# Four column groups in the first feed-forward, seven buffers for modulation weights, first weight splits issued earlier

## The chip, the cores and the metric

The kernel runs on one core of one Trainium2 chip. The metric is the device time of one launch in microseconds: a median of several runs, and beside it one execution that was profiled, to which every row below belongs. The core has a matrix engine (TensorE, written PE in the rows, with its weight loads as PEld), a vector engine (DVE), a scalar engine (ACT), GpSimd (POOL) and a sync engine (SP). Here POOL and SP mostly issue DMA transfers.

## The reference, cut to what matters

Two transformer blocks run over 512 rows of width 1024 in float32. The first has two layers. Each layer has a mixer (pooling and attention in layer 0, an mLSTM in layer 1) and a SwiGLU feed-forward, and both are modulated by columns that come from a product of the condition `c` with `ada_w`:

```python
# the modulation of one layer: six parts of 1024 columns, from ada_w[layer], a 1024 x 6144 matrix
def modulate(h, shift, scale):
    return h * (1.0 + scale[:, None, :]) + shift[:, None, :]

def swiglu(h, w1, w3, w2):                     # hidden width 2816 = 22 blocks of 128
    return (jax.nn.silu(h @ w1) * (h @ w3)) @ w2

# the second block starts from the memory as well:
x = x + memory_cross_attention(rmsnorm(x, mem_q_norm[l]), rmsnorm(mem, mem_kv_norm[l]),
                               mem_w_q[l], mem_w_kv[l], mem_w_o[l])
```

The second block (a feed-forward, a mixer, the memory attention, a second feed-forward) is not touched by the change, but a piece of its memory work is done early, inside the first block.

## The kernel before, in words

**Numbers and products.** The residual stream `x` is held as eight tiles of 128x512 (128 of the 1024 columns on the partitions, the 512 rows beside them). A float32 operand is split into a high and a low part, and each product takes three matmuls: high by high, low by high, high by low (`mm3`, L160 to L162). Weights are split the same way on the fly. SP loads a raw piece of about 1 MB into one of two buffers `raw` (L185), ACT copies the high part `wh` (L151), and DVE subtracts to get the low part `wl` (L130). PE needs `wh` for the first two matmuls of a product and `wl` for the third.

**The stages that the change touches**, in order of time: the end of layer 0's mixer with its output projection (`ev_w_out`, from about 200 us), the first feed-forward (about 255 to 640 us), and the start of the mLSTM's input projection (`od_w_in`, from about 640 us).

**Feed-forward.** `ffn` works through the 22 blocks of the hidden width in groups. For each group it makes the hidden tiles `g` of all its blocks, and then it runs the second weight matrix `w2` over the group: eight output tiles of 128x512, each the sum over the group's blocks, and each added to its tile of `x` by one DVE operation in `resid` (L908). So there are eight such additions for each group. The groups are (0,8), (8,8) and (16,6), written as first block and number. Most of the first product is done by a scheme of seven smaller products for two halves of the rows and two blocks of columns (`uprod`, matmuls L621 to L623 of 128x256), whose weight sums `sm` and inputs `h`, `hx` (`form`, L554) are made on DVE and ACT. The first four blocks' products of the first group are plain ones (`plain`, `plain_half`, L160 to L162).

**Modulation beside it.** `ada_wide` (L436) computes the modulation columns that are needed later as 16 jobs of eight tiles. POOL issues a load of 128x512 floats (256 KB) into a buffer `araw` (L449), DVE multiplies by the condition and accumulates into `acc` (L477, L479), PE sums over the partitions with four one-column matmuls (L455), and DVE writes the column (L464, L466). There are three buffers, and a load is issued two tiles ahead of its use. This work is a generator: the stages around it call it a few steps at a time (`some(side, n)`), from `evac` of the output projection, from `ffn` and from its `evac`.

**Between two stages.** `beside` (L1941) steps through the eight tiles of `modulated_forms` (L520: multiply by `rstd` on DVE, shift on ACT, split on both) or of `modulated` (L510, L512), and after every tile it lets some of the memory's work run (`fill`). The first weight splits of the stage that follows are issued once all eight tiles are done.

**The memory.** `mem_load` reads the normalised memory (`md`) back into tiles at the end of the first feed-forward, and `mem_split` splits it into `mh` and `ml`.

**What sets the order.** Python writes the instructions in the order of these loops, and a scheduler in the framework then places each on its engine's queue by its own priorities. So moving a call also moves instructions of other calls. Each engine works through its queue in order.

Of the kernel before, what the change touches and what calls it, by code (L numbers as in the profile page):

```python
# [50 lines left out]
class Net:  # L51
# [4 lines left out]
                     u=3, pm=2, acc=2, araw=3, dv=2),  # L56
        "ffn0": dict(ps=dict(wb=2, wg=2, ad=1), hx=15, w1=2, w3=4, w22=4, sm=1, g=16, s=3, u=2, c=5, acc=2, araw=3),
        "ffn": dict(ps=dict(wb=2, wg=2, ad=1), hx=15, w1=2, w3=4, w22=4, sm=1, g=16, s=4, u=4, c=6),
# [4 lines left out]
        "mem": dict(ps=dict(s=2, pt=2, po=1), r=4, k=8, q=16, p=7, pt=8),  # L63
    }

    adape = ((1, 0, 0, 0), (1, 1, 0, 0))
# [373 lines left out]
    def ada_wide(self, jobs):  # L440
# [26 lines left out]
        todo = iter([(j, k) for j in range(len(jobs)) for k in range(KT)])  # L467
        got = [load(*next(todo)) for _ in range(2)]
        for j, job in enumerate(jobs):
            acc = self.t(tag="acc")  # L470
            for k in range(KT):
                t = got.pop(0)
                jk = next(todo, None)
                if jk:
                    got.append(load(*jk))
                if k == 0:
                    nc.vector.tensor_scalar(out=acc, in0=t, scalar1=self.cond[:, 0:1], scalar2=None, op0=ALU.mult)  # L477
                else:
# [162 lines left out]

    def ffn_units(self, w1, c1, w3, c3):

        return [[dict(w=w, c=c + j * P, j=j - j0, up=up) for j in range(j0, j0 + gn, 2)
                 for up, w, c in ((False, w1, c1), (True, w3, c3))] for j0, gn in self.GROUPS]

# [34 lines left out]

    GROUPS = ((0, 8), (8, 8), (16, 6))

    def ffn(self, hs, pair, units, w2, normed, scale, after, last=None, then=None, side=None):

# [79 lines left out]

        for gi, (j0, gn) in enumerate(self.GROUPS):
            us, gs, prev = units[gi], [None] * gn, None
# [6 lines left out]
            for i, u in enumerate(us[i0:], i0):  # L774
# [25 lines left out]
                if side:  # L800
                    self.some(side, 1)
                prev = u
# [7 lines left out]
            self.mms(ps0, t0, gs, 3, gn - 2)  # L810
            t1 = next(tiles)
            ps1 = self.ps()
            self.mms(ps1, t1, gs, 0, 3)
            pss = {0: (ps0, gn - 2), 1: (ps1, 3)}

            def evac(n, ps):
                self.resid(n, ps, scale, rstd)
                if gi == len(self.GROUPS) - 1:
                    after(n)
                elif side:  # L820
                    self.some(side, 2)
            nxt = t0
            for n in range(D // P):
                if last and gi == len(self.GROUPS) - 1 and n == 6:
# [879 lines left out]

    def mem_load(self, tag="g"):
# [144 lines left out]
    def run(self):  # L1850
        a = self.a
        self.nform = self.ssn = 0
        self.eraw = self.esplit = None
        self.setup()
        self.load_x()
        pre0, hs0 = [], []
        up0, up, up1, up2 = (self.ffn_units(a[n][i], 0, a[m][j], c) for n, i, m, j, c in (
            ("ffn_w1", 0, "ffn_w3", 0, 0), ("ffn_w1", 1, "ffn_w3", 1, 0),
            ("ffn1_w_gu_2", 0, "ffn1_w_gu_2", 0, NFF * P), ("ffn2_w_gu_2", 0, "ffn2_w_gu_2", 0, NFF * P)))
        for layer in range(2):  # L1860
            ins, fill = [], []

            def evac(n, ps):
# [11 lines left out]
            if layer == 0:  # L1875
# [4 lines left out]
                with self.phase(**self.PH["ffn0"]):  # L1880
# [7 lines left out]
                    self.ss_fin()  # L1888
                    self.beside(self.modulated_forms(0, 1, pre1, ins), fill[0], (1, 0, 1, 0, 1, 0, 1, 0))

                    def then(n):
                        if n == 0:
                            self.mem_load("hx")
# [10 lines left out]
                    self.ffn(ins, lambda p: pre1[2 * p:2 * p + 2], up0, a["ffn_w2"][0], False, gate, after, then=then,  # L1904
                             side=side)
                    self.drain(side)
                    self.ss_fin()
                    self.beside(self.modulated(1, 0, pre0, hs0), fills[0], (1, 0, 1, 0, 1, 0, 1, 0))
            else:
                with self.phase(**self.PH["mlstm"]):  # L1910
                    mix = self.mlstm(hs0)
                with self.phase(**self.PH["ffn"]):
                    self.mem_load()
                    for i in range(4):
# [26 lines left out]

    def beside(self, g, fill, counts):

        for n in counts:
            next(g)
# [122 lines left out]
```

## Time and profile before

| | |
|---|---|
| runs | 2481.32 us median of 3 (2479.53 to 2482.18) |
| profiled execution | 2470.95 us, span on the core 2469.2 us |
| PE busy | 2371.5 us of the span, 96% |
| DVE, ACT, POOL busy | 1884.7, 1277.9, 229.1 us |

The profiled execution lies 10.4 us (0.4%) below the median, and 1.75 us of it lie outside the span. PE is busy nearly all the time, so what can be won or lost is the 4% in which it is idle, and the time in which it works at the lower of its clock's two levels (2.4 GHz, shown as 1.00, and 1.2 GHz, shown as 0.50). Both are found in the timeline's idle times, printed in brackets as idle before the instruction and what ended it, and in the windows' column PEclk.

### The profile page before, as it was taken

Reading aid. Unit: us, or ns where it says so; the run is one execution under the profiler, and the core shown is the slowest. Engines: PE = TensorE matmul, PEld = TensorE weight load, DVE = VectorE, ACT = ScalarE, POOL = GpSimd, SP = SyncE. Lnnn points to the kernel's source line nnn. Section 1 sums busy time; section 2 is a strip of 40 time slices with the busy share of each in tenths; the row PEclk is TensorE's granted clock in tenths of the full one; section 3 lists DMA queues with packets and bytes.
Section 4 is the critical chain, followed back from the end, with each engine's and each line's share of the span. In section 5 each row is a group of like instructions: output and inputs, shape, how many; then the busy total and the mean of one; then the engine's idle time right before and its main releaser. Section 6 shows DMA issues by size and latency. Waiting matters only on the chain.

```text
span 2469.2 us, 36653 instructions
## 1 busy us (share of the span) xinstructions
PE 2371.5 (96%) x14418; PEld 2082.1 (84%) x14418; DVE 1884.7 (76%) x3064; ACT 1277.9 (52%) x2136; POOL 229.1 (9%) x361
## 2 busy tenths in 40 slices
PE   7898899999999989999999999999999999999997
PEld 5567898979788768989898999988888788899996
DVE  7887987968687767868678787876778765978686
ACT  3564643526557756536366444455555534645453
POOL 2332112120002220000000000001011200000000
PEclk9999999999999999999999999999999999999999
DMA  9417555453333324333323333322111221233232
GB/s 303 132 54 221 170 171 192 160 186 108 118 98 95 98 67 143 113 103 103 103 86 103 103 104 103 103 94 84 52 52 52 86 86 61 94 103 110 96 102 70
DMA packets 242821, 276.37 MB, mean 112 GB/s; under 512 B 8124, under 2 KB 227132, under 8 KB 242648
## 3 DMA queue, kind: packets, MB, share of 16 engines
q1 hardware_dynamic: 232408, 240.46, 30.5%
q0 software_dynamic: 10240, 33.56, 4.2%
q8 instruction: 113, 1.85, 0.3%
q14 instruction: 60, 0.49, 0.1%
HBM read 268.47 MB, written 5.53 MB: 111 GB/s over the span
## 4 chain that ended last, share of the span: by engine, by line
PE 54%; DVE 6%; ACT 2%; issue 1%; DMA 0%; POOL 0%; DVEq 0%; ACTq 0%; POOLq 0%
PE ps L160 9%; PE ps L161 9%; PE ps L162 8%; PE ps L621 8%; PE ps L623 8%; PE ps L622 8%; DVE wl L130 1%; ACT wh L151 1%; PE ps L266 1%; PE ps L264 1%; PE ps L265 1%; PE ps L1606 1%; DVE ga L1618 0%; DVE h L130 0%; DVE w L130 0%
## 5 line engine op out<-in xcount | busy, mean ns | idle before, releaser
L151 ACT ACTIVATE wh<-raw 128x1024 fp32r<-128x1024 f32 (+1 forms) x312 | 321.0, 1030 | 457.4 <-PE ps L161 286.8
L130 DVE TENSOR_TENSOR wl<-raw,wh 128x1024 fp32r<-128x1024 f32 (+1 forms) x312 | 373.4, 1197 | 74.0 <-ACT wh L151 71.7
L161 PE MATMUL ps<-g,wh 128*128 128x512 f32 (+1 forms) x780 | 296.4, 380 | 0.0
L162 PE MATMUL ps<-g,wl 128*128 128x512 f32 (+1 forms) x748 | 288.1, 385 | 5.8 <-DVE wl L130 5.8
L160 PE MATMUL ps<-g,wh 128*128 128x512 f32 (+1 forms) x748 | 288.7, 386 | 0.9 <-ACT wh L151 0.7
L161 PE MATMUL ps<-h,wh 128*128 128x512 f32 x704 | 282.2, 401 | 1.6 <-DVE h L936 1.2
L160 PE MATMUL ps<-h,wh 128*128 128x512 f32 x688 | 278.8, 407 | 2.9 <-ACT c L151 1.2
L162 PE MATMUL ps<-h,wl 128*128 128x512 f32 x688 | 271.9, 398 | 9.3 <-DVE wl L130 9.2
L621 PE MATMUL ps<-hx,wh 128*128 128x256 f32 x960 | 272.5, 284 | 1.3 <-ACT c L151 0.7
L621 PE MATMUL ps<-h,w 128*128 128x256 f32 x960 | 272.6, 284 | 0.3 <-ACT c L151 0.3
L623 PE MATMUL ps<-h,w 128*128 128x256 f32 x960 | 271.5, 283 | 0.7 <-DVE w L130 0.7
L623 PE MATMUL ps<-hx,wl 128*128 128x256 f32 x960 | 272.2, 284 | 0.0
L622 PE MATMUL ps<-h,w 128*128 128x256 f32 x960 | 271.5, 283 | 0.0
L622 PE MATMUL ps<-hx,wh 128*128 128x256 f32 x800 | 226.7, 283 | 0.0
L151 ACT ACTIVATE c<-ps 128x256 f32<-128x256 f32 (+1 forms) x344 | 130.3, 382 | 132.9 <-PE ps L623 132.3
L621 PEld LDWEIGHTS ps<-hx,wh 128*128 128x128 f32 x960 | 184.7, 192 | 2.1 <-ACT wh L151 1.2
L621 PEld LDWEIGHTS ps<-h,w 128*128 128x128 f32 x960 | 184.4, 192 | 2.1 <-ACT c L151 1.1
L623 PEld LDWEIGHTS ps<-h,w 128*128 128x128 f32 x960 | 184.2, 192 | 1.1 <-DVE w L130 1.1
L622 PEld LDWEIGHTS ps<-h,w 128*128 128x128 f32 x960 | 184.4, 192 | 0.9
L623 PEld LDWEIGHTS ps<-hx,wl 128*128 128x128 f32 x960 | 184.8, 192 | 0.0
L162 PEld LDWEIGHTS ps<-g,wl 128*128 128x128 f32 x748 | 141.9, 190 | 35.2 <-DVE wl L130 7.7
L161 PEld LDWEIGHTS ps<-g,wh 128*128 128x128 f32 x780 | 148.0, 190 | 27.1 <-issue 0.5
(445 smaller groups left out, 5596.6 us busy)
## 6 DMA issues: line engine op xcount, KB each, us to landing
raw<-in_ffn_w_dram SPq DMA_DIRECT2D x60, 1024.0 KB
raw<-in_ffn_w_gu_dram SPq DMA_DIRECT2D x44, 1024.0 KB
araw<-in_ada_w_dram POOLq DMA_DIRECT2D x128, 256.0 KB, 4.1
araw<-in_ada_w_dram SPq DMA_DIRECT2D x16, 1024.0 KB
raw<-in_ffn_w_down_dram SPq DMA_DIRECT2D x16, 1024.0 KB
raw<-in_w_in_dram SPq DMA_DIRECT2D x14, 1024.0 KB
raw<-in_od_w_in_dram SPq DMA_DIRECT2D x12, 1024.0 KB
raw<-in_mem_w_kv_dram SPq DMA_DIRECT2D x8, 1024.0 KB
```

The lines of the kernel that those rows point to most:

```text
L130: nc.vector.tensor_tensor(out=lo, in0=src, in1=hi.bitcast(F32), op=ALU.subtract)
L151: r = nc.scalar.activation(out=out, in_=in_, func=func, **kw)
L160: mm(out, wh, xh, start=first, stop=False)
L161: mm(out, wh, xl, start=False, stop=False)
L162: mm(out, wl, xh, start=False, stop=last)
L264: mm(out, xh[:, sl], wh[:, k], start=(half == 0 and i % 2 == 0 and k == 0), stop=False)
L265: mm(out, xl[:, sl], wh[:, k], start=False, stop=False)
L266: mm(out, xh[:, sl], wl[:, k], start=False, stop=(half == 1 and i % 2 == 1 and k == 3))
L621: mm(out, wh[:, k], xh, start=(m in (1, 5) and k == 0), stop=False, skip_group_check=True)
L622: mm(out, wh[:, k], xl, start=False, stop=False, skip_group_check=True)
L623: mm(out, wl[:, k], xh, start=False, stop=(k == 3), skip_group_check=True)
L1606: nc.tensor.matmul(ps[:, c * P:(c + 1) * P], lh[:, c * P:(c + 1) * P], rh[:, c * P:(c + 1) * P], start=True, stop=True)
```

## The change

- The first feed-forward's groups become (0,6), (6,6), (12,6), (18,4): `GROUPS0`. The other feed-forwards keep `GROUPS`. The number of matmuls is the same.
- `ada_wide` has seven `araw` buffers and loads six tiles ahead. It yields after every tile (before: every second one), and its callers ask for other numbers of steps. The room comes from `g`, which goes from 16 buffers to 12.
- `beside` takes a place and a function. Ahead of tile 5 (of 8) it issues the first weight load and split of the first feed-forward (`plain_begin`), ahead of tile 5 the first two of `od_w_in`, and ahead of tile 6 those of layer 1's feed-forward.
- `form` gives the modulated tiles of the first feed-forward buffers of `h` first and of `hx` later (`formskip`), and the memory's high parts lie in `hx`.

```diff
-        "ffn0": dict(... hx=15, ... g=16, s=3, u=2, c=5, acc=2, araw=3),
+        "ffn0": dict(... hx=15, ... g=12, s=3, u=2, c=5, acc=2, araw=7),
...
+    GROUPS = ((0, 8), (8, 8), (16, 6))
+    GROUPS0 = ((0, 6), (6, 6), (12, 6), (18, 4))
...
-        got = [load(*next(todo)) for _ in range(2)]
+        got = [load(*next(todo)) for _ in range(6)]
...
-                if tail and k == 1:
+                if tail and k == 0:
                     ps = sums(tail[0])
-                elif tail and k == 5:
+                elif tail and k == 3:
                     result(ps, *tail[1])
-                if k % 2:
-                    yield
+                yield
...
-        n = self.nform % 32
+        n = (self.nform + self.formskip) % 32
...
+    def plain_begin(self, us):
+        self.uload(us[0])
+        self.plain_half(us[0], 0)
...
                 if side:
-                    self.some(side, 1)
+                    self.some(side, 2)
...
-            self.mms(ps0, t0, gs, 0, 3)
+            k3 = min(3, gn - 2)
+            self.mms(ps0, t0, gs, 0, k3)
...
                 elif side:
-                    self.some(side, 2)
+                    self.some(side, 3)
...
-    def mem_tiles(self, tag="g"):
+    def mem_tiles(self, tag="hx"):
...
                 if layer == 0:
-                    self.some(side, 2)
+                    self.some(side, (4, 4, 3, 3, 3, 3, 4, 4)[n])
...
-                    self.beside(self.modulated_forms(0, 1, pre1, ins), fill[0], (1, 0, 1, 0, 1, 0, 1, 0))
+                    self.beside(self.modulated_forms(0, 1, pre1, ins), fill[0], (1, 0, 1, 0, 1, 0, 1, 0), 5,
+                                lambda: self.plain_begin(up0[0]))
...
-                             side=side)
+                             side=side, groups=self.GROUPS0)
+                    self.formskip = 0
...
-                    self.beside(self.modulated(1, 0, pre0, hs0), fills[0], (1, 0, 1, 0, 1, 0, 1, 0))
+                    self.beside(self.modulated(1, 0, pre0, hs0), fills[0], (1, 0, 1, 0, 1, 0, 1, 0), 5,
+                                lambda: [self.begin(a["od_w_in"][0], 0, 256, i) for i in range(2)])
...
-                    self.beside(self.modulated_forms(1, 1, pre1, ins), fill[0], (4,) * 8)
+                    self.beside(self.modulated_forms(1, 1, pre1, ins), fill[0], (4,) * 8, 6,
+                                lambda: self.plain_begin(up[0]))
...
-        for n in counts:
+        for i, n in enumerate(counts):
+            if i == at:
+                begin()
             next(g)
```

The queues differ from about 190 us to about 700 us of the trace. Ahead of that and behind it every engine's order is as it was, that of layer 1's feed-forward included. In the changed kernel line numbers are higher by three to seven.

The PE queue in the output projection of layer 0, before: the one-column sums (L455) of a modulation job stand between the matmuls of the seventh output tile `ps_455`.

```order
L161 MATMUL ps_447_1874<-h_361_1494,wh_437_1819 128x512
L162 MATMUL ps_447_1874<-h_360_1493,wl_438_1820 128x512
L160 MATMUL ps_455_1921<-h_285_1235,wh_445_1870 128x512
L161 MATMUL ps_455_1921<-h_286_1236,wh_445_1870 128x512
L455 MATMUL ps_452_1910<-tabs_73,acc_430_1794 128x1 x4
L162 MATMUL ps_455_1921<-h_285_1235,wl_446_1871 128x512
L160 MATMUL ps_455_1921<-h_303_1297,wh_445_1870 128x512
```

And of the change: they stand ahead of the sums of squares (L323), behind all eight output tiles and a part of the memory's product.

```order
L164 MATMUL ps_457_1942<-g_375_1519,wh_455_1938 128x256
L165 MATMUL ps_457_1942<-hx_371_1515,wl_456_1939 128x256
L458 MATMUL ps_461_1974<-tabs_73,acc_434_1802 128x1 x4
L323 MATMUL ps_473_2005<-ssq_382_1560,tabs_73 128x512
L324 MATMUL ps_473_2005<-sq_458_1968,tabs_73 128x512
L163 MATMUL ps_482_2030<-hx_368_1512,wh_479_2023 128x256
```

The sums, of the third job in both, moved back by the last two output tiles and some of the memory's matmuls. What they wait for is still the last of eight DVE accumulations into `acc`.

The DVE queue at the start of the first feed-forward, before: `g` by `rstd` is the modulated tile (L520, four more of them stand ahead of these rows), `hx` its low part, and `wl_2173` the low part of the first weights.

```order
L520 TENSOR_TENSOR g_2001<-g_2001,rstd_2012 128x512
L130 TENSOR_TENSOR hx_2024<-g_1993,hx_2023 128x512
L520 TENSOR_TENSOR g_2003<-g_2003,rstd_2012 128x512
L130 TENSOR_TENSOR hx_2062<-g_1995,hx_2061 128x512
L520 TENSOR_TENSOR g_2005<-g_2005,rstd_2012 128x512
L130 TENSOR_TENSOR hx_2068<-g_1997,hx_2067 128x512
L520 TENSOR_TENSOR g_2007<-g_2007,rstd_2012 128x512
L130 TENSOR_TENSOR wl_2173<-raw_2170,wh_2172 128x1024
L130 TENSOR_TENSOR hx_2108<-g_1999,hx_2107 128x512
```

And of the change (three L522, the former L520, stand ahead; `h` is now the low part of a modulated tile, and `wl_2148` is the low part of the first weights):

```order
L522 TENSOR_TENSOR g_1995<-g_1995,rstd_2008 128x512
L522 TENSOR_TENSOR g_1997<-g_1997,rstd_2008 128x512
L133 TENSOR_TENSOR wl_2148<-raw_2145,wh_2147 128x1024
L133 TENSOR_TENSOR h_2020<-g_1989,h_2019 128x512
L522 TENSOR_TENSOR g_1999<-g_1999,rstd_2008 128x512
L133 TENSOR_TENSOR h_2058<-g_1991,h_2057 128x512
L522 TENSOR_TENSOR g_2001<-g_2001,rstd_2008 128x512
```

The first weights' low part moved from behind eight multiplications and three splits to behind five multiplications, with no split ahead of it.

The DVE queue at the start of the mLSTM, before (behind `rstd`, three L510 and one L512): `h` by `rstd` (L510) and `h` from `mod` (L512) make one modulated tile each, and `wl_6338` is the first low part of `od_w_in`.

```order
L510 TENSOR_TENSOR h_6023<-h_6023,rstd_6176 128x512
L512 SCALAR_TENSOR_TENSOR h_6224<-h_5959,mod_85,h_6223 128x512
L510 TENSOR_TENSOR h_6054<-h_6054,rstd_6176 128x512
L510 TENSOR_TENSOR h_6087<-h_6087,rstd_6176 128x512
L512 SCALAR_TENSOR_TENSOR h_6229<-h_5990,mod_85,h_6228 128x512
L510 TENSOR_TENSOR h_6116<-h_6116,rstd_6176 128x512
L512 SCALAR_TENSOR_TENSOR h_6268<-h_6023,mod_85,h_6267 128x512
L510 TENSOR_TENSOR h_6171<-h_6171,rstd_6176 128x512
L512 SCALAR_TENSOR_TENSOR h_6273<-h_6054,mod_85,h_6272 128x512
L130 TENSOR_TENSOR wl_6338<-raw_6335,wh_6337 128x1024
L512 SCALAR_TENSOR_TENSOR h_6310<-h_6087,mod_85,h_6309 128x512
```

And of the change (behind `rstd` and three L512; `wl_6368` is the same low part; L512 and L514 are the former L510 and L512):

```order
L514 SCALAR_TENSOR_TENSOR h_6243<-h_6033,mod_85,h_6242 128x512
L512 TENSOR_TENSOR h_6103<-h_6103,rstd_6232 128x512
L514 SCALAR_TENSOR_TENSOR h_6280<-h_6051,mod_85,h_6279 128x512
L512 TENSOR_TENSOR h_6128<-h_6128,rstd_6232 128x512
L133 TENSOR_TENSOR wl_6368<-raw_6365,wh_6367 128x1024
L514 SCALAR_TENSOR_TENSOR h_6285<-h_6076,mod_85,h_6284 128x512
```

Before it stood behind eight L510 and five L512 after `rstd`, and now it stands behind five and two.

## Rows read from the trace of the kernel before

**Rows 1.** The page, section 1: busy time, share of the span, instructions of each engine.

```profile
PE 2371.5 (96%) x14418; PEld 2082.1 (84%) x14418; DVE 1884.7 (76%) x3064; ACT 1277.9 (52%) x2136; POOL 229.1 (9%) x361
```

**Rows 2.** Timeline of PE, 190 to 670 us: start, duration, instruction, idle before, releaser.

```profile
192.12 1.22 PE L1689 MATMUL ps<-s,tabs 128*128 128x256 f32 x2 [3.02 <-ACT s L151]
...
232.64 1.78 PE L455 MATMUL ps<-tabs,acc 128*128 128x1 f32 x8 [4.22 <-DVE acc L479]
...
262.94 0.79 PE L162 MATMUL ps<-hx,wl 128*128 128x512 f32 x1 [3.65 <-DVE wl L130]
...
387.55 0.79 PE L162 MATMUL ps<-g,wl 128*128 128x512 f32 x1 [2.01 <-DVE wl L130]
...
408.34 0.39 PE L623 MATMUL ps<-h,wl 128*128 128x256 f32 x1 [2.02 <-DVE wl L130]
...
527.35 0.79 PE L162 MATMUL ps<-g,wl 128*128 128x512 f32 x1 [2.26 <-DVE wl L130]
...
548.65 0.39 PE L623 MATMUL ps<-h,wl 128*128 128x256 f32 x1 [2.47 <-DVE wl L130]
...
660.98 0.79 PE L162 MATMUL ps<-h,wl 128*128 128x512 f32 x1 [4.74 <-DVE wl L130]
```

**Rows 3.** The tile `araw`: its load and use, DVE's waits for it, landing times.

```profile
L449 POOL DMA_DIRECT2D araw<-in_ada_w_dram x128: 536/536/823, 184.0 to 543.3; - x128
...
  DMA araw<-in_ada_w_dram: 56.0, 35
...
DMA to landing us min/median/max: 3.0/4.1/7.4
```

**Rows 4.** Timeline of DVE, 240 to 408 us.

```profile
250.32 0.75 DVE L479 SCALAR_TENSOR_TENSOR acc<-araw,cond,acc 128x512 f32<-128x512 f32 x1 [1.89 <-DMA araw<-in_ada_w_dram]
...
384.34 0.75 DVE L479 SCALAR_TENSOR_TENSOR acc<-araw,cond,acc 128x512 f32<-128x512 f32 x1 [3.05 <-DMA araw<-in_ada_w_dram]
...
406.40 0.75 DVE L479 SCALAR_TENSOR_TENSOR acc<-araw,cond,acc 128x512 f32<-128x512 f32 x1 [2.40 <-DMA araw<-in_ada_w_dram]
407.07 1.22 DVE L130 TENSOR_TENSOR wl<-sm,wh 128x1024 fp32r<-128x1024 f32 x1
```

**Rows 5.** Windows in which PE works below full clock: busy times, PEclk, DMA share.

```profile
233.00:241.00 8.00, 8.00 (x26) 6.58 (x27) 5.71 (x10) 4.61 (x8) 1.94 (x4) 0.59 0.92 302
263.00:268.00 5.00, 5.00 (x14) 3.99 (x15) 5.00 (x10) 4.45 (x9) 0.00 (x0) 0.62 0.18 43
388.00:394.00 6.00, 6.00 (x17) 4.67 (x17) 4.67 (x8) 0.00 (x0) 2.49 (x5) 0.57 0.62 175
528.00:534.00 6.00, 6.00 (x17) 4.67 (x16) 4.52 (x7) 0.00 (x0) 2.69 (x5) 0.58 0.63 187
550.00:554.00 4.00, 4.00 (x23) 4.00 (x23) 4.00 (x7) 1.81 (x3) 0.00 (x0) 0.57 0.00 0
661.00:667.00 6.00, 6.00 (x16) 4.72 (x17) 5.33 (x15) 0.72 (x1) 0.00 (x0) 0.57 0.50 155
```

**Rows 6.** Windows of three other stretches, the same columns, GB/s last.

```profile
250.00:290.00 40.00, 34.36 (x180) 29.27 (x179) 39.68 (x68) 26.70 (x45) 3.22 (x6) 0.91 0.44 140
390.00:560.00 170.00, 161.46 (x1082) 149.59 (x1081) 138.39 (x220) 68.11 (x118) 30.09 (x56) 0.96 0.56 181
402.00:406.00 4.00, 4.00 (x36) 4.00 (x35) 1.48 (x3) 0.77 (x2) 1.07 (x2) 1.00 1.06 372
```

**Rows 7.** Timeline of DVE at the start of the mLSTM.

```profile
651.23 1.90 DVE L510 TENSOR_TENSOR h<-h,rstd 128x512 f32<-128x512 f32 x3
653.04 0.74 DVE L512 SCALAR_TENSOR_TENSOR h<-h,mod,h 128x512 fp32r<-128x512 f32 x1
...
659.72 1.21 DVE L130 TENSOR_TENSOR wl<-raw,wh 128x1024 fp32r<-128x1024 f32 x1
```

**Rows 8.** Line L908: nanoseconds min/median/max, first and last start.

```profile
L908 DVE SCALAR_TENSOR_TENSOR x<-ps,mod,x x31: 740/746/752, 199.1 to 639.9; 128x512 f32<-128x512 f32 x31
```

**Rows 9.** Timeline of SP: the memory's reload.

```profile
597.39 1.90 SPq L1708 DMA_DIRECT2D hx<-md  x4
```

More of the change, by code (lines that the diff above doesn't have):

```diff
@@ L56 @@
                      u=3, pm=2, acc=2, araw=3, dv=2),
-        "ffn0": dict(ps=dict(wb=2, wg=2, ad=1), hx=15, w1=2, w3=4, w22=4, sm=1, g=16, s=3, u=2, c=5, acc=2, araw=3),
+        "ffn0": dict(ps=dict(wb=2, wg=2, ad=1), hx=15, w1=2, w3=4, w22=4, sm=1, g=12, s=3, u=2, c=5, acc=2, araw=7),
         "ffn": dict(ps=dict(wb=2, wg=2, ad=1), hx=15, w1=2, w3=4, w22=4, sm=1, g=16, s=4, u=4, c=6),
@@ L640, in uout2, with ffn_units @@
         return u["wb"][:, 0:S // 2]
-    def ffn_units(self, w1, c1, w3, c3):
+    def ffn_units(self, w1, c1, w3, c3, groups=GROUPS):
         return [[dict(w=w, c=c + j * P, j=j - j0, up=up) for j in range(j0, j0 + gn, 2)
-                 for up, w, c in ((False, w1, c1), (True, w3, c3))] for j0, gn in self.GROUPS]
+                 for up, w, c in ((False, w1, c1), (True, w3, c3))] for j0, gn in groups]
     def unit_steps(self, us):
@@ L679, in ubegin, with ffn @@
             self.uload(us[1])
-    GROUPS = ((0, 8), (8, 8), (16, 6))
-    def ffn(self, hs, pair, units, w2, normed, scale, after, last=None, then=None, side=None):
+    def ffn(self, hs, pair, units, w2, normed, scale, after, last=None, then=None, side=None,
+            groups=GROUPS):
         nc, H = self.nc, S // 2
@@ L764, in plain @@
             return forms
-        for gi, (j0, gn) in enumerate(self.GROUPS):
+        for gi, (j0, gn) in enumerate(groups):
             us, gs, prev = units[gi], [None] * gn, None
@@ L806, in ffn @@
             ps0 = self.ps()
-            self.mms(ps0, t0, gs, 0, 3)
+            k3 = min(3, gn - 2)
+            self.mms(ps0, t0, gs, 0, k3)
             self.uprod(prev, forms, 4)
             out2(prev, gs)
-            self.mms(ps0, t0, gs, 3, gn - 2)
+            self.mms(ps0, t0, gs, k3, gn - 2)
             t1 = next(tiles)
             ps1 = self.ps()
-            self.mms(ps1, t1, gs, 0, 3)
-            pss = {0: (ps0, gn - 2), 1: (ps1, 3)}
+            self.mms(ps1, t1, gs, 0, k3)
+            pss = {0: (ps0, gn - 2), 1: (ps1, k3)}
             def evac(n, ps):
                 self.resid(n, ps, scale, rstd)
-                if gi == len(self.GROUPS) - 1:
+                if gi == len(groups) - 1:
                     after(n)
                 elif side:
-                    self.some(side, 2)
+                    self.some(side, 3)
             nxt = t0
             for n in range(D // P):
-                if last and gi == len(self.GROUPS) - 1 and n == 6:
+                if last and gi == len(groups) - 1 and n == 6:
                     last(nxt, tiles, gs, rstd)
@@ L1703, in mem_rows, with mem_load @@
         return d[2 * i * P:2 * (i + 1) * P, :].rearrange("(k p) c -> p k c", p=P)
-    def mem_load(self, tag="g"):
+    def mem_load(self, tag="hx"):
         self.mem_tiles(tag)
@@ L1853, in run @@
         self.eraw = self.esplit = None
+        self.formskip = 15
         self.setup()
@@ L1856, in run @@
         pre0, hs0 = [], []
-        up0, up, up1, up2 = (self.ffn_units(a[n][i], 0, a[m][j], c) for n, i, m, j, c in (
-            ("ffn_w1", 0, "ffn_w3", 0, 0), ("ffn_w1", 1, "ffn_w3", 1, 0),
+        up, up1, up2 = (self.ffn_units(a[n][i], 0, a[m][j], c) for n, i, m, j, c in (
+            ("ffn_w1", 1, "ffn_w3", 1, 0),
             ("ffn1_w_gu_2", 0, "ffn1_w_gu_2", 0, NFF * P), ("ffn2_w_gu_2", 0, "ffn2_w_gu_2", 0, NFF * P)))
+        up0 = self.ffn_units(a["ffn_w1"][0], 0, a["ffn_w3"][0], 0, self.GROUPS0)
         for layer in range(2):
@@ L1888, in run @@
                     self.ss_fin()
-                    self.beside(self.modulated_forms(0, 1, pre1, ins), fill[0], (1, 0, 1, 0, 1, 0, 1, 0))
+                    self.beside(self.modulated_forms(0, 1, pre1, ins), fill[0], (1, 0, 1, 0, 1, 0, 1, 0), 5,
+                                lambda: self.plain_begin(up0[0]))
                     def then(n):
                         if n == 0:
-                            self.mem_load("hx")
+                            self.mem_load()
                         elif 2 <= n < 6:
@@ L1912, in run @@
                 with self.phase(**self.PH["ffn"]):
-                    self.mem_load()
+                    self.mem_load("g")
                     for i in range(4):
@@ L1940, in run, with beside @@
                      self.normed_next(None, None), last=self.finish)
-    def beside(self, g, fill, counts):
-        for n in counts:
+    def beside(self, g, fill, counts, at, begin):
+        for i, n in enumerate(counts):
+            if i == at:
+                begin()
             next(g)
```

## The prediction, written before the changed kernel ran

> **What bounds the kernel now.** I read the page first: PE is busy for 96% of the span [rows 1], so a change that leaves the matmuls as they are can only gain from the other 4% and from slow clock. Then I read PE's idle times in the stretch whose order changes, about 190 to 700 us. Up to the start of the mLSTM eight of them exceed 2 us [rows 2]. Six end at a `wl`, the low part of weights, that DVE delivers late, one at DVE's accumulation into `acc`, one at the memory's load. Next I asked what DVE did before those moments: at 384.34 and 406.40 it had just stood idle for 3.05 and 2.40 us until an `araw` load landed, and the `wl` that PE waits for is queued behind it, as at 407.07 [rows 4]. The second joint between groups, at 522 to 549 us, repeats the pattern. Over the kernel DVE sat idle 56.0 us in 35 such waits, and a load takes 4.1 us to land, up to 7.4 [rows 3]. Last come the windows behind the gaps: PE works there at a mean clock of 0.57 to 0.62, mostly at the lower of its two levels [rows 5]. The 2.02 us gap at 408.34 cost no clock: the stretch before it ran at 1.00 and no such window follows [rows 2, 6].
>
> A window's loss is its length times what its clock lacks of 1.00: 233 to 241 loses 8 x 0.41 = 3.3 us, 263 to 268 1.9, 388 to 394 2.6, 528 to 534 2.5, 550 to 554 1.7, 661 to 667 2.6.
>
> **The change part by part.** The sum is made in differences against the profiled execution (2470.95 us) and then laid on the median, 10.4 us higher.
>
> *Seven buffers, six loads ahead, start.* The first four extra loads, 1 MB, are issued by POOL just before and beside the memory's own load on SP, on which PE waits 3.02 us at 192.12 [rows 2]. At the 372 GB/s that a loaded stretch reaches [rows 6] they take 2.8 us. That delay is between 0 (all issued behind) and 2.8 (all ahead). POOL needs 0.54 us for each issue [rows 3], so about half of them can be ahead: -1.5.
>
> *Seven buffers, output projection.* The third job's one-column sums move behind the eighth output tile, and DVE's waits for loads go. The 4.22 us gap at 232.64, the 3.3 us of clock behind it, and DVE's own 1.89 us wait at 250.32, which stands between the last output tile and `rstd` [rows 4], make `rstd` earlier by 9.4 us. The bounds are 7.5 (PE's part alone) and 11.6 (with the small waits of DVE and PE between 240 and 254 us).
>
> *First weights of the first feed-forward earlier.* PE waits 3.65 us for them at 262.94, and loses 1.9 on clock. I cost the gain at nothing. DVE is busy for 39.68 of the 40 us from 250 to 290 [rows 6], and no instruction of that stretch is removed. Taking the low part of the first weights forward lets PE start earlier and then wait for what was pushed back. The new wait should be at the weights of the first half-product (`uprod`), some 35 us behind `rstd`: about 3 us of gap that replaces 3.65, with perhaps clock lost later than before. I take -1.7 for it, that is one window's 1.9 less a little; the bounds are -4 and +5.5 (both losses gone). The output projection and this together: 9.4 - 1.7 = +7.7.
>
> *The joints between groups.* With six loads queued, a load has several steps to land, where 4.1 us had to fit into two. DVE should then reach `wl` in time. What goes is 2.01 + 2.6 + 2.02 at the first joint and 2.26 + 2.5 + 2.47 + 1.7 at the second, 15.5 us [rows 2, 5]. There are three joints afterwards. A fourth group adds eight additions of 0.75 us on DVE [rows 8], 6 us in all, and they lie beside PE's matmuls as long as DVE has idle time: it had 170 - 138.39 = 31.6 us in 390 to 560 [rows 6]. A `w2` tile over six blocks holds 18 matmuls instead of 24. At the rate of rows 5 (17 in 6 us at 0.57, so 0.20 us each) that is 3.6 us of PE, while DVE has 0.75 for the addition, three quarters of 1.22 for `wl` and up to three accumulations of 0.75: 3.9. So cover is thin there, and I allow one new gap of 2.0 us with a clock loss of 2.6 at even odds: -2.3. Net +13.2; the bounds are 15.5 and, if DVE is late at all three joints by that much, 15.5 - 3 x 4.6 = 1.7.
>
> *First weights of the mLSTM earlier.* Their low part began at 659.72, behind eight multiplications and five other steps after `rstd` [rows 7], and PE waited 4.74 us [rows 2]. Now five and two stand ahead. Three multiplications of 0.6 (1.90 for three) and three steps of 0.66 (653.04 to 653.70) are 3.8 us, and a part of the 2.6 us of clock comes with it, since less of an idle stretch is left: +4.8. DVE is not the limit here, because behind these tiles PE has products that need no more of them. The bounds are 2 and 7.3 (4.74 + 2.6).
>
> *The memory's tiles in `hx`.* The reload at 597.39 [rows 9] now has to wait for later products of the last group to let go of `hx`, and the memory's splits come up ahead of work of the last group on ACT and DVE. Those issued behind it on SP are the next `w2` pieces. I take -1.5; the bounds are 0 and -4 (a gap such as those of rows 2 of 2 us, with 1.7 to 2.6 of clock).
>
> *Layer 1's `plain_begin`, `formskip`, `GROUPS` as an argument.* No queue behind 700 us differs, so nothing.
>
> Sum: -1.5 + 7.7 + 13.2 + 4.8 - 1.5 = 22.7 us faster, 2481.3 - 22.7 = 2458.6; I say **2458 us** (2448 for an execution like the profiled one).
>
> **The rivals.**
>
> *The loads stay late.* The loaded stretch moves 372 GB/s with the DMA engines wholly busy [rows 6]. If `araw` lands late because a raw piece occupies the engines, and not because only two loads are in flight, six in flight wait together. Then the projection and the joints keep about half of what they lose, and the gain falls by some 10 to 12: 2469. For it: the waits in rows 4 stand next to raw loads. Against it: the stretch from 390 to 560 moved 181 GB/s on average [rows 6], under half of what it reaches, so a longer queue can level the peaks.
>
> *Raw weights come late instead.* More loads outstanding on POOL's queue slow each raw piece on SP's. If the two queues share evenly, a piece of 1 MB beside two loads (0.5 MB) is through after 1.5 MB, about 4.1 us at 372 GB/s, and beside four or more after 2 MB, 5.5 us: 1.4 us later wherever PE waits for a piece. At five places (the start, the three joints, the mLSTM's start) that is 7 us: 2465. Against it: once the first six are issued, a new load comes no faster than DVE frees a buffer, so the loads on their way are not more per microsecond than before. The Trainium skill's page "DMA: Bandwidth & Descriptors", section "Queues, rings and completion order", states the even sharing: each DMA engine takes turns between the queues that have work for it, a packet at a time. The trace has no row that separates the two queues; it shows only that both together fill the engines.
>
> *DVE becomes the bound (slower).* This is decided at the joints, by DVE's work on a `w2` tile against PE's. If the sums and splits of the next group's weights, which also lie in these eight tiles, cannot get ahead, DVE has 8 x 3.9 = 31 us and about 10 us for them against PE's 8 x 3.6 = 29: 12 us late at each of three joints, 36, and 3 x 2.6 of clock, 44 in all. Against the 15.5 that go and about 10 from the other stages the kernel would be 18 us slower: 2499. It begins to decide once DVE is late by more than 8 us a joint. For it: DVE was at 81% in 390 to 560 and will be near 89% (138.39 + 4 in about 160). Against it: PE's products in the first part of each group leave DVE time, and DVE was ahead of PE in most of that stretch.
>
> *The gain is given back.* PE arrives earlier at the end of the feed-forward or the mLSTM, and waits there for loads that are not earlier. PE's waits for raw loads themselves are none among rows 2 (one is for the memory), so I give it little: 2479.
>
> **How the numbers follow.** The forecast has 0.60, the late loads 0.22, the late raw weights 0.06, the gain given back 0.06, the DVE bound 0.06. The likeliest case by itself spans 2446 to 2468, from its bounds (not all at once). The range with eight chances in ten has to take in most of the late loads: 2445 to 2472. Measurements of this kernel tell 0.2%, 5 us, from no change. Faster by more than that: forecast, late loads and late raw weights, 0.88. Within it: 0.06. Slower: 0.06.
>
> **What would show it.** In the changed profile DVE's waits for `araw` fall from 56 us to under 25. PE's gaps at the `wl` of the joints are gone or under 1 us, and the windows at about 0.57 behind them read 0.9 or more. The sums at the end of the projection wait for nothing. A gap of 2 to 4 us stands at the first half-product of the feed-forward instead. The first `wl` of `od_w_in` begins some 5 us behind `rstd`, not 9. DVE's busy time rises by 6 us, PE's falls by the clock's part, 10 or so. I am wrong if PE still waits for `wl` in the joints with DVE fully busy ahead of it (the bound), or with DVE waiting for `araw` (the late loads).

## The result, and the profile after

The changed kernel takes 2442.35 us (2441.84 to 2443.47, four runs), the kernel before 2480.43 in the runs beside it; the ratio is 0.9848, with an interval from 0.9831 to 0.9865. So it is 38 us faster, where 23 were forecast, and it lies 2.7 us below the range. The profiled executions are 2470.95 and 2443.47 us, only 27.5 apart. The forecast's mechanism can be compared with that, and the remaining 10 us need a cause of their own.

First, PE's idle times in the same stretch, as in [rows 2] (start, duration, instruction, idle before, releaser). Of the six waits for `wl` in those rows, a part of one is left, at the mLSTM's start, and the wait of 4.22 us for `acc` is gone. The wait of 1.99 us for `wh` is new:

```profile
192.23 2.08 PE L1696 MATMUL ps<-s,tabs 128*128 128x256 f32 x4 [3.40 <-ACT s L154]
...
250.94 0.50 PE L164 MATMUL ps<-h,wh 128*128 128x512 f32 x1 [0.56 <-DVE h L133]
...
282.04 0.39 PE L623 MATMUL ps<-hx,wh 128*128 128x256 f32 x1 [1.99 <-ACT wh L154]
...
629.86 0.50 PE L163 MATMUL ps<-h,wh 128*128 128x512 f32 x1 [1.17 <-ACT c L154]
631.19 0.55 PE L165 MATMUL ps<-h,wl 128*128 128x512 f32 x1 [0.60 <-DVE wl L133]
```

The tile `araw` after, as in [rows 3]. DVE's waits for loads fell from 56.0 us to 5.7, although a load takes no less time to land; POOL has issued the last load 18 us sooner:

```profile
L452 POOL DMA_DIRECT2D araw<-in_ada_w_dram x128: 536/536/727, 183.7 to 525.7; - x128
...
  DMA araw<-in_ada_w_dram: 5.7, 7
...
DMA to landing us min/median/max: 3.0/4.4/7.9
```

Windows after (columns as in [rows 5, 6]). From 330 to 620 us, with three joints between groups in it, PE is busy for 289.27 of 290 us at full clock. DVE has 86% of that stretch, so it had room. From 244 to 284 DVE is saturated, as in [rows 6]. The clock falls in six places from 150 to 960 us, none of them at a joint (second block):

```profile
244.00:284.00 40.00, 36.97 (x193) 30.47 (x192) 39.95 (x68) 28.68 (x46) 3.39 (x7) 0.95 0.43 144
330.00:620.00 290.00, 289.27 (x1962) 267.62 (x1961) 250.46 (x396) 143.18 (x240) 39.10 (x73) 1.00 0.52 170
```
```profile
191.00:198.00 7.00, 5.53 (x12) 3.98 (x13) 4.53 (x7) 2.15 (x4) 3.22 (x6) 0.51 0.95 345
252.00:256.00 4.00, 3.85 (x9) 2.55 (x10) 4.00 (x9) 4.00 (x9) 0.00 (x0) 0.58 0.21 73
283.00:287.00 4.00, 4.00 (x20) 3.99 (x21) 3.48 (x6) 1.17 (x3) 0.46 (x1) 0.57 0.96 337
631.00:635.00 4.00, 3.81 (x10) 2.99 (x11) 4.00 (x7) 1.48 (x3) 0.79 (x5) 0.57 0.22 37
853.00:861.00 8.00, 6.91 (x24) 5.42 (x25) 4.90 (x7) 4.01 (x7) 0.35 (x1) 0.57 0.40 131
867.00:874.00 7.00, 7.00 (x14) 3.73 (x13) 3.14 (x5) 2.58 (x4) 0.31 (x1) 0.51 0.00 0
```

A window's length times what its clock lacks of 1.00 is here either 1.7 us (4 x 0.42) or 3.4 (8 x 0.43): 15.4 us in the six. The same count gives 23.9 us for the kernel before in that stretch. Idle time inside a window is counted in it, unlike in the prediction, whose windows begin behind the gaps.

The mLSTM's start, as in [rows 7]: the first `wl` of `od_w_in` begins 4.34 us after the first multiplication by `rstd` here (L512, the former L510), 8.49 us before.

```profile
625.58 1.89 DVE L512 TENSOR_TENSOR h<-h,rstd 128x512 f32<-128x512 f32 x3
...
629.92 1.22 DVE L133 TENSOR_TENSOR wl<-raw,wh 128x1024 fp32r<-128x1024 f32 x1
```

Two more waits of PE change behind it. A second long wait for a `wl` (first row, before) is gone; 0.48 us at a later matmul is what is left there. And a short one for the mLSTM's `v` grows (second row before, third after, the same matmul):

```profile
695.18 0.50 PE L162 MATMUL ps<-h,wl 128*128 128x512 f32 x1 [2.36 <-DVE wl L130]
728.96 0.39 PE L264 MATMUL ps<-wh,h 128*128 128x256 f32 x1 [0.19 <-DVE v L130]
698.02 0.39 PE L267 MATMUL ps<-wh,h 128*128 128x256 f32 x1 [1.33 <-DVE v L133]
```

Where the time came from, by the start of PE's matmul of the same number in each execution (the count is the same in all; the third profile of the kernel before is told of below):

```
matmul   what starts there           before   before, 3rd   after
 720     behind the memory's load     201.8      203.1      203.6
1120     first half-products          292.5      294.6      283.3
3484     mLSTM's projection           655.5      659.2      629.9
3660     behind its first tiles       707.1      711.9      675.0
4740     end of the mLSTM             908.9      915.6      881.2
gain by stage against before:         -1.7, +10.9, +16.4, +6.5, -4.5
gain by stage against before, 3rd:    -0.4, +11.7, +18.1, +7.5, -2.4
forecast:                             -1.5,  +7.7, +11.7, +4.8,  0
```

The forecast's third entry is 13.2 for the joints less 1.5 for the memory's tiles.

### The profile page after: what moved, and what is told of

It reads as the page before. It is cut to its first block, busy times and chain, and to the rows that moved or that the text cites. A ratio compares the mean times of both kernels' runs of the same rounds, so it can differ in the third digit from the quotient of the medians.

```text
span 2441.5 us, 36682 instructions
## 1 busy us (share of the span) xinstructions
PE 2368.0 (97%) x14418; PEld 2076.8 (85%) x14418; DVE 1892.1 (77%) x3080; ACT 1280.9 (52%) x2144; POOL 227.5 (9%) x361
## 4 chain that ended last, share of the span: by engine, by line
PE 76%; DVE 14%; ACT 5%; issue 2%; DMA 2%; POOL 1%; SPq 0%; DVEq 0%; ACTq 0%; POOLq 0%
PE ps L163 12%; PE ps L164 12%; PE ps L165 12%; PE ps L623 11%; PE ps L625 11%; PE ps L624 11%; DVE wl L133 2%; ACT wh L154 1%; DVE qk L1149 1%; PE ps L267 1%; PE ps L269 1%; PE ps L268 1%; DVE acc L408 1%; DVE h L133 1%; PE ps L1073 1%
## 5 line engine op out<-in xcount | busy, mean ns | idle before, releaser
L154 ACT ACTIVATE wh<-raw 128x1024 fp32r<-128x1024 f32 (+2 forms) x320 | 322.8, 1010 | 450.1 <-PE ps L164 268.1
L133 DVE TENSOR_TENSOR wl<-raw,wh 128x1024 fp32r<-128x1024 f32 (+2 forms) x320 | 375.2, 1173 | 72.3 <-ACT wh L154 69.6
L164 PE MATMUL ps<-h,wh 128*128 128x512 f32 x732 | 293.0, 401 | 2.4 <-DVE h L943 1.2
L163 PE MATMUL ps<-h,wh 128*128 128x512 f32 x720 | 291.3, 407 | 2.9 <-ACT c L154 1.2
L623 PE MATMUL ps<-hx,wh 128*128 128x256 f32 x800 | 227.2, 284 | 3.1 <-ACT wh L154 2.4
L625 PE MATMUL ps<-hx,wl 128*128 128x256 f32 x800 | 227.0, 284 | 0.0
L623 PE MATMUL ps<-h,w 128*128 128x256 f32 x760 | 215.4, 284 | 0.0
L625 PE MATMUL ps<-h,w 128*128 128x256 f32 x760 | 215.0, 283 | 0.0
L624 PE MATMUL ps<-h,w 128*128 128x256 f32 x720 | 203.6, 283 | 0.0
L624 PE MATMUL ps<-hx,wh 128*128 128x256 f32 x680 | 192.8, 284 | 0.0
L164 PEld LDWEIGHTS ps<-h,wh 128*128 128x128 f32 x732 | 139.8, 191 | 35.5 <-DVE h L133 4.0
L624 PE MATMUL ps<-h,wh 128*128 128x256 f32 x600 | 170.0, 283 | 0.0
L164 PEld LDWEIGHTS ps<-g,wh 128*128 128x128 f32 x780 | 146.9, 188 | 26.9 <-DVE g L133 0.5
L165 PEld LDWEIGHTS ps<-h,wl 128*128 128x128 f32 x720 | 137.1, 190 | 37.7 <-DVE wl L133 6.4
L163 PEld LDWEIGHTS ps<-h,wh 128*128 128x128 f32 x720 | 137.2, 191 | 34.0 <-ACT h L154 2.4
L163 PEld LDWEIGHTS ps<-g,wh 128*128 128x128 f32 x716 | 134.6, 188 | 28.0 <-ACT wh L154 0.9
```

The costliest lines, as they stand in the source:

```text
L133: nc.vector.tensor_tensor(out=lo, in0=src, in1=hi.bitcast(F32), op=ALU.subtract)
L154: r = nc.scalar.activation(out=out, in_=in_, func=func, **kw)
L163: mm(out, wh, xh, start=first, stop=False)
L164: mm(out, wh, xl, start=False, stop=False)
L165: mm(out, wl, xh, start=False, stop=last)
L623: mm(out, wh[:, k], xh, start=(m in (1, 5) and k == 0), stop=False, skip_group_check=True)
```

## The experiments

**The kernel before, again.** Two more profiles of it, with no edit. 

> The kernel before, unchanged, to profile another execution of it. The profiled execution of before lies 10 us under its median, that of the change on its median. Theory A (the places of the change): in ordinary executions before loses some 10 us more at the very joints of 190 to 700 us (longer waits for araw, or a lower clock behind them), so a profile at about 2480 us shows PE idle and slow clock in 190 to 700 us that exceed those of the first profile by 8 us or more. Theory B (elsewhere): 190 to 700 us is as in the first profile within 3 us, and the 10 us lie ahead of or behind it. If this profile falls at 2471 again, nothing is told by it.

The timed executions gave 2476.69 us, and the profiled one 2482.54. It loses 34.1 us of clock from 150 to 960 us, and it is 7.8 us behind the first profile at matmul 2820 (second joint), of which 2.8 came up to 205 us. Behind the mLSTM it is 11.4 us behind. So about half of it lies between 205 and 565 (5 us). From 190 us to matmul 3660, PE's idle time grew by 3.2 us and the loss by 6.8, more than A's 8 together, but only 7 us show in the starts of the matmuls, and another 3.7 lie in the mLSTM. A holds in part.

> A third profile of the kernel before. So far its profiles took 2470.95 and 2482.54 us with 23.9 and 34.1 us of clock lost between 150 and 960 us, and timed executions lie between. If the executions differ by how much clock their gaps cost, and PE's waits are the same, a profile at T us has a loss that grows by about one for each microsecond of T: 28 to 31 us at 2476 to 2478. If it is the length of the waits that differs, the loss stays at 24 to 26 and the idle time from 150 to 960 us grows from 42.6 us instead.

It took 2477.8 us, just the median of the kernel before, with 32.4 us of clock lost and 44.8 us of idle time above 0.3 us, where the first profile had 42.6. The loss grew by 8.5 us (it counts idle time in slow windows, so not all of it is PE's), and the idle time by 2.2, where the span grew by 6.9. So the clock is what differs most, by a little more than the 28 to 31 us of loss that were expected. The gap at the end of the first joint shows it, with the window behind it, in the first, the second and the third profile: 2.02, 2.43 and 4.99 us of idle time [rows 2], and a loss of 0, 1.7 and 3.4 us.

```profile
408.00:412.00 4.00, 3.66 (x30) 3.66 (x31) 4.00 (x8) 2.45 (x4) 0.54 (x1) 1.00 0.28 81
```
```profile
413.43 0.39 PE L623 MATMUL ps<-h,wl 128*128 128x256 f32 x1 [2.43 <-DVE wl L130]
```
```profile
414.00:418.00 4.00, 4.00 (x23) 4.00 (x22) 4.00 (x7) 2.45 (x4) 0.54 (x1) 0.57 0.36 113
```
```profile
411.82 0.58 PE L623 MATMUL ps<-h,wl 128*128 128x256 f32 x1 [4.99 <-DVE wl L130]
```
```profile
409.00:417.00 8.00, 5.18 (x27) 5.18 (x28) 7.12 (x11) 2.45 (x4) 1.07 (x2) 0.57 0.26 79
```

Here the waits differ in length too. At the second joint they don't: 2.26 us at 527.35 of the first profile [rows 2] with a loss of 3.4 (first row), and 2.27 with a loss of 1.7 in the third.

```profile
526.00:534.00 8.00, 6.65 (x17) 5.22 (x18) 6.48 (x10) 0.00 (x0) 3.22 (x6) 0.57 0.61 179
```
```profile
530.95 0.50 PE L162 MATMUL ps<-g,wl 128*128 128x512 f32 x1 [2.27 <-DVE wl L130]
```
```profile
532.00:536.00 4.00, 4.00 (x12) 3.14 (x11) 3.96 (x6) 0.00 (x0) 1.36 (x3) 0.57 0.57 175
```

In all, 39 further executions of the kernel before took 2473.0 to 2483.3 us (median 2477.9), with mean granted clocks of 0.981 to 0.986. None was as short as the one whose rows the forecast rests on.

**The change, again.** No edit. 

> The changed kernel, unchanged, for the scatter of its executions and a second profile. Ten executions of the kernel before spread over 8 us and more (2474.2 to 2482.5). Theory A (each gap of PE costs 1.7 or 3.4 us of slow clock, by chance, and the change takes gaps away): the changed kernel spreads over less than 5 us, about 2440 to 2445, and its second profile has 12 to 19 us of clock loss in 150 to 960 us, against 23.9 and 34.1 in the two profiles of before. Theory B (the scatter is the chip's, not the gaps'): a spread of 8 us here as well.

2442.98 us (2436.57 to 2446.22), with 15.4 us of clock lost in that stretch. The spread of nearly 10 us is against A's forecast: fewer gaps did not make the executions more alike. The loss itself is as A put it. The eight timed executions of the change have clocks of 0.989 to 0.991.

**Two loads ahead.**

```diff
-        "ffn0": dict(... g=12, ... araw=7),
+        "ffn0": dict(... g=12, ... araw=3),
...
-        got = [load(*next(todo)) for _ in range(6)]
+        got = [load(*next(todo)) for _ in range(2)]
```

> The change with three buffers and two loads ahead as before; groups, steps per call and early weight splits as in the change. Theory A (depth of the loads is the main cause): DVE's waits for araw come back to 40 us or more from 6, PE waits again for wl at the joints, and the time is 2460 to 2475 us. Theory C (the finer steps and the four groups did it): within 5 us of the change, 2440 to 2448.

2463.32 us, 21 above the change: the depth of the loads, as theory A said. DVE's waits for `araw` are 44.0 us, and short waits of PE stand at the groups, mostly for ACT's `wh` and DVE's addition rather than, as expected, for `wl`:

```profile
  DMA araw<-in_ada_w_dram: 44.0, 33
```
```profile
353.88 0.50 PE L163 MATMUL ps<-g,wh 128*128 128x512 f32 x1 [1.32 <-ACT wh L154]
...
540.08 0.47 PE L163 MATMUL ps<-g,wh 128*128 128x512 f32 x1 [1.14 <-DVE x L915]
```

From matmul 1120 to 3484 this kernel is 13.1 us longer than the change (7.7 of them more idle time of PE), up to 1120 5.8.

**Four loads ahead.**

```diff
-        "ffn0": dict(... araw=7),
+        "ffn0": dict(... araw=5),
...
-        got = [load(*next(todo)) for _ in range(6)]
+        got = [load(*next(todo)) for _ in range(4)]
```

> The change with five buffers and four loads ahead instead of seven and six. Two ahead measured 2463.3, six 2442.4. If a load has to cover only its landing of some 4 us and up to 7, four are enough: 2442 to 2446. If the gain goes with the depth: about 2450 to 2455.

2443.68 us. Four are as good as six; DVE's waits are 12.9 us, and PE's at the joints stay away.

**Three groups, two ahead.** On top of the run with two ahead:

```diff
-        "ffn0": dict(... g=12, ...),
+        "ffn0": dict(... g=16, ...),
...
-    GROUPS0 = ((0, 6), (6, 6), (12, 6), (18, 4))
+    GROUPS0 = ((0, 8), (8, 8), (16, 6))
```

> Groups (0,8), (8,8), (16,6) as before, 16 buffers g, three araw buffers and two loads ahead as before; finer steps and early weight splits as in the change. Against the run with two loads ahead and four groups it tells the price of the fourth group. My sum: eight additions on DVE that cost nothing where PE is late anyway, so within 5 us of that run. Rival (a joint has a price of its own, 4.6 us each): 4 to 8 us faster than that run. Theory C (finer steps alone are the gain): within 5 us of the change here too.

2459.58 us, 3.7 less than with four groups. So no gain of the fourth group by itself shows. Whether it costs a little is open, since the runs overlap (2456.9 to 2460.7 and 2459.2 to 2464.9). What it does is make room for the loads: four tiles of `g` fewer are the four of `araw` more. Three groups with deeper loads would need more tiles than either kernel holds in this stage, and no run tried them.

**Finer steps alone.** The kernel of the last run, and without the early splits:

```diff
         for i, n in enumerate(counts):
-            if i == at:
-                begin()
             next(g)
```

> Three groups, three buffers, two loads ahead and no early splits, as before; only the finer steps with their places for the sums, and the memory's tiles in hx. With the early splits this was 2459.6 us, 18.5 under before; the early splits were worth 5.2 in the change. So 2463 to 2467 if they are worth the same here, which puts 12 to 15 us on the finer steps alone. Rival: the finer steps work only together with the early splits: 2472 or more.

2465.36 us, in the range forecast, and 11.5 under the kernel before in the runs beside it. So some 12 us are gained without deeper loads, groups or early splits, though DVE waits for `araw` 64.9 us here. The finer steps and the places of the sums are most of what is left of the change. The memory's tiles in `hx` and `formskip` are in this kernel too, and no run separates them.

**Coarse steps with the deep loads.**

```diff
-                if tail and k == 0:
+                if tail and k == 1:
                     ps = sums(tail[0])
-                elif tail and k == 3:
+                elif tail and k == 5:
                     result(ps, *tail[1])
-                yield
+                if k % 2:
+                    yield
...
-                    self.some(side, (4, 4, 3, 3, 3, 3, 4, 4)[n])
+                    self.some(side, 2)
```

(`ffn` asks for 1 and 2 again instead of 2 and 3.)

> The change with the former coarse steps: ada_wide yields every second tile and its callers ask for the former numbers; the sums and results at the former places. Four groups, seven buffers, six ahead and early splits stay. If depth is enough: within 4 us of the change, 2440 to 2447. If the finer steps have a part of their own (the third job's sums behind the output tiles above all): 2450 or more, with the wait of the one-column sums for acc back in the projection.

2449.42 us, 6.4 more than the change, between the two forecasts. The sums' wait is not in the projection but later in the feed-forward, at 465 us, and a wait of the half-products for ACT stands 100 us ahead of it:

```profile
364.88 0.39 PE L624 MATMUL ps<-h,wh 128*128 128x256 f32 x1 [2.75 <-ACT c L154]
```
```profile
465.20 1.01 PE L458 MATMUL ps<-tabs,acc 128*128 128x1 f32 x6 [1.65 <-DVE acc L482]
```

Its profile is 10.9 us longer than the change's between matmuls 1120 and 3484, 6.2 of them idle time of PE, and part of that comes back later, where its clock lost less than the change's. So beside deep loads the finer steps show 6.4 us, not the 11.5 of the run before.

**No early splits.** The change without `begin()`, the edit of the run with the finer steps alone. 

> The change without the early weight splits in beside (neither for the first feed-forward, nor for the mLSTM, nor for layer 1's feed-forward). My sum gives 4.8 us for the mLSTM's and nothing for the first feed-forward's, where DVE is saturated: 2445 to 2450 us, with the gap of 3 to 5 us at the first wl of od_w_in back. Rival: the first feed-forward's is worth its 3.65 us of wait and 1.9 of clock as well: 2450 to 2455.

2447.53 us, 5.2 more. The gap at `od_w_in` is back at its old size, and up to the mLSTM only 1.5 us are lost, though the first feed-forward's weights come 2.44 us late. The wait for `v` is back at 0.20 us. It is 1.31 to 1.36 in all profiles with early splits and 0.19 or 0.20 in all without:

```profile
253.47 0.80 PE L165 MATMUL ps<-h,wl 128*128 128x512 f32 x1 [2.44 <-DVE wl L133]
```
```profile
636.86 0.80 PE L165 MATMUL ps<-h,wl 128*128 128x512 f32 x1 [4.74 <-DVE wl L133]
```

**A staggered start.**

```diff
-        got = [load(*next(todo)) for _ in range(6)]
+        got = [load(*next(todo)) for _ in range(2)]
...
-                jk = next(todo, None)
-                if jk:
-                    got.append(load(*jk))
+                for _ in range(2 if j == 0 and k < 4 else 1):
+                    jk = next(todo, None)
+                    if jk:
+                        got.append(load(*jk))
```

> The change, but only two loads at the start, and two for each of the first four tiles, until six are ahead. It tests the price of the burst at the start, which I put at 1.5 us: the memory's load then lands as in the kernel before, PE's wait near 192 us falls from 3.4 to 3.0 or below, and the time is 2440 to 2442. Rival: the wait falls under the point at which it costs clock, and 3.4 more come with it: 2437 to 2439. Other rival: the first jobs come later and nothing is gained: 2442 to 2444.

2443.14 us, no gain. But the edit did not take the burst away. POOL issues seven loads in a row here as in the change (first row the change, second this run), so the run says nothing of the burst's price:

```profile
183.75 3.91 POOL L452 DMA_DIRECT2D araw<-in_ada_w_dram  x7 [8.63 <-DVE h L133]
186.03 3.91 POOL L452 DMA_DIRECT2D araw<-in_ada_w_dram  x7 [8.63 <-DVE h L133]
```
```profile
194.97 1.65 PE L1697 MATMUL ps<-s,tabs 128*128 128x256 f32 x3 [3.74 <-ACT s L154]
```

The number of buffers sets the burst, and the other profiles tell its price. The memory's load comes in four pieces, and ACT squares them for PE's sums. Where POOL starts with three loads, ACT squares the third and the fourth piece without a pause (first row, the kernel before; at most 0.04 us in six profiles). Where it starts with five or seven, ACT waits another 1.5 to 1.7 us for the fourth in all six profiles (second and third row, the change). PE then waits for that piece 0.25 us at most (last row):

```profile
191.44 1.21 ACT L151 ACTIVATE s<-hx 128x512 f32<-128x512 f32 x2 [3.86 <-DMA hx<-in_memT_dram]
```
```profile
191.54 0.63 ACT L154 ACTIVATE s<-hx 128x512 f32<-128x512 f32 x1 [4.24 <-DMA hx<-in_memT_dram]
193.87 0.63 ACT L154 ACTIVATE s<-hx 128x512 f32<-128x512 f32 x1 [1.69 <-DMA hx<-in_memT_dram]
```
```profile
194.55 2.07 PE L1696 MATMUL ps<-s,tabs 128*128 128x256 f32 x4 [0.25 <-ACT s L154]
```

PE's longer wait, for the third piece, is 3.02 to 4.08 us in the six profiles with three loads and 3.40 to 4.56 in the five with seven. These overlap, so no price of the burst shows in it.

## Why the prediction was wrong, step by step

**The step that failed: laying the sum on the median, "10.4 us higher".** That carries the difference between one execution and the others over unchanged, as if it lay where nothing changes. The profiled execution was a short one, mainly because its gaps had cost little clock: 23.9 us, against 32.4 and 34.1 in two others. PE's busy time for the same matmuls shows it without idle time: 2371.5 us in that profile [rows 1], 7.2 more in the third (first row), which is all of the 6.9 us between the two:

```profile
PE 2378.7 (96%) x14418; PEld 2087.7 (84%) x14418; DVE 1884.9 (76%) x3064; ACT 1278.8 (52%) x2136; POOL 228.7 (9%) x361
PE 2368.0 (97%) x14418; PEld 2076.8 (85%) x14418; DVE 1892.1 (77%) x3080; ACT 1280.9 (52%) x2144; POOL 227.5 (9%) x361
```

The change (second row) lies 10.7 us under the third profile in this, as forecast ("10 or so"), but only 3.5 under the first. So the 5 us that the sum is short of the first profile's 27.5 are what is left of two misses: some 24 us of idle time went where it had 13, and 3.5 us of clock where it had 10.

About half of what the two other profiles are longer lies where the change acts (3.4 of 6.9 and 5.0 of 11.6 us, between matmuls 720 and 3660). Most of the rest lies at the memory's load and in the mLSTM, where the changed kernel's profiles show the larger losses too. Against the profile at the median, 2477.8 us, the change gains 34 us; against the first, 27.5. Of the miss of 16 us (2458 to 2442) the sum has about 5, and this step the rest. Of its 10.4 us, 6.9 are the distance to that profile, and 3.5 come from the three runs it was laid on, which were long (2481.3, where 39 others have 2477.9) for no cause that a run shows. What stays open is why the same gap costs 0, 1.7 or 3.4 us of clock. Its length alone doesn't say: in the first profile 2.01 us at 387.55 cost 3.4 and 2.02 us at 408.34 nothing.

**"Cost no clock" at 408.34** was read off one execution and taken as a property of the place. It cost 1.7 and 3.4 in the two others.

**The joints: mechanism right, term too small.** 13.2 less 1.5 against 16.4 in the first profile and 18.1 in the third. The 2.3 held back for a new gap was not needed (330 to 620 us above), and the row that stands for the additions, as in [rows 8], shows the eight more that PE does not wait for:

```profile
L915 DVE SCALAR_TENSOR_TENSOR x<-ps,mod,x x39: 742/751/752, 200.6 to 614.3; 128x512 f32<-128x512 f32 x39
```

The depth is the main cause, as forecast: 21 us of the whole go when only two loads are ahead. But the sum gave all of the joints to the depth. The finer steps, which it did not price by themselves, are worth 6.4 us beside deep loads and, with the moved tiles, some 12 alone.

**The projection and the first weights: 7.7 against 10.9 to 11.7.** `rstd` came earlier by nearly the upper bound of 11.6: its L345 starts at 244.33, the same step before at 253.79, 9.5 us sooner, although matmul 720 started 1.7 later, so 11.2 in this stage. The new wait stands where it was forecast, at the first half-product, with 1.99 us instead of about 3. That the early weights are worth nothing there, because DVE is saturated, held: 1.5 us without them.

**The mLSTM's start: 4.8 against 6.5 to 7.5.** `wl` comes 4.15 us sooner, as counted (3.8). The clock's part is not what the sum lacked: a window of 1.7 us is left at 631. PE's idle time in this stage fell by 5.9 us, and about 2 of these are a second wait for `wl` (2.36 us before, 0.48 left) that the sum did not have. Without the early splits 5.2 us are lost.

**The start: -1.5.** The delay is there, with nearly that size (1.5 to 1.7 us for the memory's last piece), but PE waits for it no more than 0.25 us. The rest of the 1.7 that this stage is longer than in the first profile is mainly clock: the window at the memory's load lost 3.4 us, and 1.7 in that profile. The Trainium skill's page "DMA: Bandwidth & Descriptors", section "Queues, rings and completion order", states that each DMA engine takes turns between the queues that have work for it; the traces agree so far, as more loads on POOL's queue make SP's last piece later.

**The memory's tiles: -1.5.** PE's only wait above 0.3 us at the end of the feed-forward is 0.5, at 594.88, so this was too much.

**What the sum left out:** 2.4 to 4.5 us were given back in the mLSTM. One part is the wait for `v`, 1.33 us where 0.19 stood: PE, earlier with `wl`, waits there instead. Against the first profile, two windows near 855 and 870 us also lost 3.4 us each, where that one lost 1.7 each; against the third they are equal.

**The rivals.** The loads did not stay late (5.7 us), and DVE did not become the bound (86%). Raw weights did not come late either: at 282.04, PE's longest new wait, ACT's copy had itself waited 1.62 us for DVE. Of the gain given back a little came true, 1.1 us, for `v` and not for a load.

## What to carry to other kernels

A small load that feeds a side job on an in-order engine has to be issued far enough ahead to land before its turn, since what waits behind it on that queue may be what the matrix engine needs; buffers for this can be worth a costlier tiling elsewhere. Price a stall with the clock it costs, and read that clock from more than one execution of the kernel. Where the one profile lies well off the median, ask first what made it so, before laying a sum on either. And before an experiment is read, look in its trace whether the queue that its edit should change has changed.

## What the runs showed of the hardware

Between 150 and 960 us the loss behind a gap of PE came in two sizes, 1.7 and 3.4 us, in all five profiles of the two kernels, and a wait at the same place of the same program took one or the other, or none, by execution: 2.26 and 2.27 us at the second joint cost 3.4 and 1.7. Executions of one program differ by about 10 us of 2440 to 2480, and a kernel with about half as many slow windows spread as widely. So the clock is not shown to be the whole of that spread.

Five or seven loads of 256 KB, issued by POOL beside and behind SP's four pieces of the memory, kept ACT waiting for the last piece 1.5 to 1.7 us longer than three such loads did, in all twelve profiles. The third piece showed no clear delay.
